# Where tiles begin in the on-chip memory, and when a small 0/1 matrix is loaded, in a one-layer hybrid decoder kernel

## The chip, the cores and the metric

The kernel runs on one core of a Trainium2 chip. A core has a matrix engine (PE, with its weight loads shown apart as PEld), three engines for elementwise work (DVE, ACT, POOL) and SP, on whose queue this kernel issues every DMA. Each engine takes its instructions in the order in which they were written into its own stream, and waits for the others by semaphores. The metric is the device time of one execution in microseconds; the kernel before took 1067.3 us (median of 3 runs, 1065.59 to 1068.7).

## The reference

The input `x` is 2048 tokens of 1024 channels. It is normalised and multiplied by one weight matrix whose 3328 columns feed four mixers of 256 channels, each with a gate:

```
h = _rms_norm(x, pre_g)
proj = jnp.einsum('bsd,de->bse', h, w_in)
aq, ak, av, ag, bu, bv, bg, cx, cg, dq, dk, dv, dg = jnp.split(proj, N_IN_SLICES, axis=-1)
ya = _dilated_mixture(heads(aq), heads(ak), heads(av))   # 4 heads, dilations 1, 4, 16
yb = _spatial_gating(bu, bv, sgu_g, sgu_w, sgu_b)
yc = _multiscale_pool(cx, pool_w, pool_scale)
yd = _retention(dq, dk, dv, ret_g)
y = jnp.concatenate([ya * jax.nn.silu(ag), yb * jax.nn.silu(bg),
                     yc * jax.nn.silu(cg), yd * jax.nn.silu(dg)], axis=-1)
y = jnp.einsum('bse,ed->bsd', y, w_out)
return x + _rms_norm(y, post_g)
```

The dilated mixture computes softmax attention three times per head (dilations 1, 4, 16) and adds the three results, each weighted per token by its share of the softmax denominators.

## The kernel before, in words

Every large product is made in three matmuls on values rounded to the matrix engine's reduced fp32 format (`F32R`): high part by high part, high by low, low by high. So an operand `x` becomes a pair: `hh` and `hl` for the normalised input (transposed, 8 blocks of 128 channels by 512 tokens), `w[:, 0]` and `w[:, 1]` for weights.

Phase 1 goes over the sequence in two halves of 1024 tokens. `prologue` normalises and transposes the half into `hh` and `hl`; then come the projections, in the order of the loop at the end of phase 1 (attention values, retention, attention queries and keys, spatial gating, pooling, attention gates). `proj_t` writes a 128-channel by 512-token block (tile `ps_t`) with `hh`/`hl` streamed through the array and weights loaded into it, 24 matmuls of 512 columns; `proj_m` writes token by channel (tile `ps_m`) with the roles swapped, matmuls of 256 columns. Results that phase 2 needs go to DRAM (`qk`, `vd`, `agd`, `yb`).

Phase 2 runs attention for two pairs of heads. `attention(p, tab)` loads queries `q2`, keys `k2a`, `k2b` and values `att_v` of a head into seven rotating buffers (tag `m8`), and `branch` works through one dilation: scores (`ps_s`), bias and row minimum on DVE (`att_p`, line 649), exponential on ACT (651), transposes into `ps_pt`, a split into `pt_hi` on ACT (658) and `pt_lo` on DVE (659), and values times probabilities (`ps_o`). `weigh` turns the three sets of row statistics into weights `wt`; it uses a small tile `eh`. `combine` spreads these weights over the 64 channels of a head by a matmul with a constant matrix of zeros and ones, `sel` (32 rows, 8 blocks of 128 columns), and sums the dilations. `out_weights` loads and splits rows of `w_out` (`wo_raw`, 128x1024). During attention of the second pair, `partial` computes the output projection of six of the eight blocks for 9 of the 16 token tiles (`ps_out`). Phase 3 finishes all 16 tiles (`final`): remaining blocks, the second normalisation, the residual, and the store.

The 0/1 matrix comes between the two pairs: two DMAs of 32x512 values into buffers of the attention probabilities (tag `pr`), each followed by a rounding copy on DVE into `sel` (lines 887 to 890).

The order on each engine isn't the order in the source: the program is recorded with a scheduler that simulates a timeline, so an instruction can be moved in its engine's stream past independent ones. Buffers are tiles of pools; a tile with a tag waits until the earlier holder of its buffer has been read for the last time. The addresses follow from the order and size of the pools: on the left side `const` (only `ident`), `big` (four buffers of 16 KB: `hh`, `hl`, later `wo` and one attention result), `small`, then the pools of a phase. So the size of `const` shifts `big` and all that follows it, and the size of `small` shifts all that follows `small`.

Of the kernel before, what the change touches and what calls it, by code (L numbers as in the profile page):

```python
# [9 lines left out]
F32 = mybir.dt.float32  # L10
F32R = mybir.dt.float32r
# [7 lines left out]
P = 128  # L19
SEQ = 2048  # L20
DM = 1024
KT = DM // P
GRP = 512
# [10 lines left out]
C_ID, C_DEC, C_ZETA, C_XI, C_CD, C_INVP, C_CNT, C_SEL, C_MIX = 0, 128, 640, 896, 1152, 1408, 1410, 1442, 2466  # L34
# [6 lines left out]
B_PR, B_PT = 6, 3  # L41
# [47 lines left out]
def hymba(ctx: ExitStack, tc: tile.TileContext, x, pre_g, w_in, sgu_g, sgu_w, sgu_b, pool_w,  # L89
          pool_scale, ret_g, w_out, post_g, cmix, catt, out, dbg=None, npart=9, spread=(0.3, 0.95)):  # L90
    nc = tc.nc
    V, A, G, T, D = nc.vector, nc.scalar, nc.gpsimd, nc.tensor, nc.sync

    def r32(ap):
        return ap.bitcast(F32)
# [7 lines left out]
    cp = ctx.enter_context(tc.tile_pool(name="const", bufs=1))  # L103
    big = ctx.enter_context(tc.tile_pool(name="big", bufs=4))
    small = ctx.enter_context(tc.tile_pool(name="small", bufs=2))
# [13 lines left out]
    ya_d = [scratch(f"ya{g}", [P, 2, GRP]) for g in range(NG)]  # L119

    ident = cp.tile([P, P], F32, name="ident")

    def rsqrt(o, v, n):

# [416 lines left out]
    p3 = ctx.enter_context(tc.tile_pool(name="p3", bufs=1, side="right", reuse_waits="tile"))  # L541
# [15 lines left out]
    def attention(p, tab):  # L557
        o01 = (big if p == 0 else po).tile([P, 2, SEQ], F32, tag="big" if p == 0 else "o01", name="att_o01")
        o2 = po.tile([P, SEQ], F32, tag="o2", name="att_o2")
        o = [o01[:, 0], o01[:, 1], o2]  # L560
        wt = pc.tile([P, 3, 2, 2, 2, 8], F32, tag="wt", bufs=1, name="wt")
        for s in range(2):
            h = 2 * p + s
            rows = slice(s * HD, (s + 1) * HD)
            other = slice((1 - s) * HD, (2 - s) * HD)
            q2 = pm.tile([P, SEQ], F32R, tag="m8", bufs=7, name="q2")
            k2a = pm.tile([P, SEQ], F32R, tag="m8", bufs=7, name="k2a")
            k2b = pm.tile([P, SEQ], F32R, tag="m8", bufs=7, name="k2b")
            D.dma_start(r32(q2[rows]), qk_d[0][p][rows, 0])
            D.dma_start(r32(q2[other]), qk_d[0][p][rows, 1])  # L570
            for z in (rows, other):
                D.dma_start(r32(k2a[z]), qk_d[1][p][rows, 0])
                D.dma_start(r32(k2b[z]), qk_d[1][p][rows, 1])
            for b, dil in enumerate(DILS):
                vt = pm.tile([P, 16, 2 * HD], F32R, tag="m8", bufs=7, name="att_v")
                dst = r32(vt)
                if dil == 1:
                    src = v_d[h].rearrange("(n t c) d -> c t n d", c=4, t=32)
                    for c in range(4):
                        D.dma_start(dst[c * 32:(c + 1) * 32], src[c])  # L580
                elif dil == 4:
                    D.dma_start(dst.rearrange("q (j c) d -> q j (c d)", j=4),
                                v_d[h].rearrange("(j q c) d -> q j (c d)", j=4, c=4))
                else:
                    D.dma_start(dst.rearrange("q r d -> q (r d)"), v_d[h].rearrange("(q r) d -> q (r d)", r=16))
                qb = q2
                if dil != 1:
                    qb = pm.tile([P, SEQ], F32R, tag="m8", bufs=7, name="q2b")
                    if dil == 4:
                        src = r32(q2).rearrange("p (j k c i) -> p c j k i", j=4, c=4, i=8)  # L590
                        dst = qb.rearrange("p (j c k i) -> p c j k i", j=4, c=4, i=8)
                        for c in range(4):
                            (V if c < 3 else G).tensor_copy(dst[:, c], src[:, c])
                    else:
                        V.tensor_copy(qb.rearrange("p (r w i) -> p r w i", r=16, i=8),
                                      r32(q2).rearrange("p (w r i) -> p r w i", r=16, i=8))
                if dil == 1:
                    sv = p2.tile([P, 3, 2, 16], F32, tag="sv", bufs=2, name="sv")
                    raw = p2.tile([64, P], F32, tag="sT", bufs=1, name="sraw")
                    D.dma_start(raw, st_d[h].rearrange("b z (n q) -> (b z n) q", q=P))  # L600
                    branch(h, dil, qb, k2a, k2b, vt, tab, o[b], sv[:, b])
                    weigh(sv, raw, wt[:, :, :, s])
                    continue
                st = p2.tile([P, 2, 16], F32, tag="stat", bufs=2, name="att_st")
                branch(h, dil, qb, k2a, k2b, vt, tab, o[b], st)
                keep_stats(h, b, dil, st)
        return o01, o2, wt
# [121 lines left out]
    def keep_stats(h, b, dil, st):  # L729

        pt = ps2.tile([P, GRP], F32, tag="t", bufs=N_T, name="ps_st")
        transpose(pt[:32, :P], st.rearrange("p z n -> p (z n)"))
        sT = p2.tile([32, P], F32, tag="sT", bufs=1, name="sT")
        V.tensor_copy(sT, pt[:32, :P])
        for z in range(2):
            dst, src = st_d[h][b, z], sT[z * 16:(z + 1) * 16]
            if dil == 4:
                for j in range(4):
                    D.dma_start(dst.rearrange("(j k c i) -> j c k i", j=4, k=16, c=4)[j],
                                src[j * 4:j * 4 + 4].rearrange("c (k i) -> c k i", i=8))  # L740
            else:
                D.dma_start(dst.rearrange("(w r i) -> r w i", r=16, i=8), src.rearrange("r (w i) -> r w i", i=8))

    def weigh(sv, raw, w):

        pt = ps2.tile([P, GRP], F32, tag="t", bufs=N_T, name="ps_sv")
        transpose(pt[:, :64], raw, 64)
        V.tensor_copy(sv[:, :2].rearrange("q b z n -> q (b z n)"), pt[:, :64])
        nm = small.tile([P, 16], F32, tag="nm", name="nm")
        V.tensor_tensor(nm, sv[:, 0, 0], sv[:, 1, 0], ALU.min)  # L750
        V.tensor_tensor(nm, nm, sv[:, 2, 0], ALU.min)
        df = small.tile([P, 3, 16], F32, tag="df", name="df")
        V.tensor_tensor(df, sv[:, :, 0], nm.unsqueeze(1).broadcast_to([P, 3, 16]), ALU.subtract)
        ew = small.tile([P, 3, 16], F32, tag="ew", name="ew")
        A.activation(ew, df, AF.Exp, scale=-1.0)
        V.tensor_tensor(df, ew, sv[:, :, 1], ALU.mult)
        V.tensor_tensor(nm, df[:, 0], df[:, 1], ALU.add)
        V.tensor_tensor(nm, nm, df[:, 2], ALU.add)
        V.reciprocal(nm, nm)
        V.tensor_tensor(ew, ew, nm.unsqueeze(1).broadcast_to([P, 3, 16]), ALU.mult)  # L760
        eh = small.tile([P, 3, 16], F32R, tag="eh", name="eh")
        V.tensor_copy(eh, ew)
        V.tensor_copy(w[:, :, :, 0], r32(eh).rearrange("q b (g n) -> q b g n", g=2))
        for b in range(3):
            V.tensor_tensor(w[:, b, :, 1], ew[:, b].rearrange("q (g n) -> q g n", g=2),
                            r32(eh[:, b]).rearrange("q (g n) -> q g n", g=2), ALU.subtract)
# [111 lines left out]
    pc = ctx.enter_context(tc.tile_pool(name="pc", bufs=1, side="right", reuse_waits="tile"))  # L878
    sel = pc.tile([32, 8, P], F32R, name="sel")
    with ExitStack() as c2:  # L880
        pm = c2.enter_context(tc.tile_pool(name="pm", bufs=1, reuse_waits="tile"))
        p2 = c2.enter_context(tc.tile_pool(name="p2", bufs=1, reuse_waits="tile"))
        ps2 = c2.enter_context(tc.tile_pool(name="ps2", bufs=2, space=PSUM, reuse_waits="tile"))
        tab = pm.tile([P, T_HEAD], F32, name="tab")
        D.dma_start(tab, catt)
        o = attention(0, tab)
        for z in range(2):
            raw = p2.tile([P, 4, P], F32, tag="pr", bufs=B_PR, name="sel_raw")[:32]
            D.dma_start(raw, cmix[:32, C_SEL + z * GRP:C_SEL + (z + 1) * GRP].rearrange("r (n m) -> r n m", m=P))
            V.tensor_copy(sel[:, z * 4:z * 4 + 4], raw)  # L890
        for i in (1, 2, 3):
            out_weights(i, V if i == 2 else G)
        combine(0, o, ps2, "t", False, range(0, SEQ, GRP), G)
        o = attention(1, tab)
        for t in range(npart):
            with tc.issue_after(marks[int(len(marks) * (t + spread[0]) / npart * spread[1])]):
                partial(t)
        out_weights(0, G)
# [13 lines left out]
    for i, t in enumerate(full):  # L912
        n = -(-len(have) // (len(full) - i))
# [30 lines left out]
```

## Time and profile before

| | |
|---|---|
| median of 3 runs | 1067.3 us (1065.59 to 1068.7) |
| the profiled execution | 1072.46 us, its span 1070.8 us |
| mean granted clock of the matrix engine | 0.977 |
| busy: PE, PEld, DVE, ACT, POOL | 95%, 81%, 49%, 35%, 21% of the span |
| HBM traffic | 127.9 MB, 119 GB/s over the span |

Phase 1 lasts to about 690 us of the span, the attention of the two head pairs to about 940, phase 3 to the end. A page lists, for each engine, busy time and groups of instructions; "idle before" is the time that the engine waited ahead of a group, with what ended the wait. The chain of waits is followed back from the last instruction: each piece ends by releasing the next. The windows view gives busy time by stretch, and the granted clock (PEclk, 1.00 is full speed). In the timeline an x behind a tile counts merged instructions, and brackets hold the idle time and its releaser. SPq rows are the issue of a DMA, not its transfer.

### The profile page before, as it was taken

Reading aid. Unit: us, or ns where it says so; the run is one execution under the profiler, and the core shown is the slowest. Engines: PE = TensorE matmul, PEld = TensorE weight load, DVE = VectorE, ACT = ScalarE, POOL = GpSimd, SP = SyncE. Lnnn points to the kernel's source line nnn. Section 1 sums busy time; section 2 is a strip of 40 time slices with the busy share of each in tenths; the row PEclk is TensorE's granted clock in tenths of the full one; section 3 lists DMA queues with packets and bytes.
Section 4 is the critical chain, followed back from the end, with each engine's and each line's share of the span. In section 5 each row is a group of like instructions: output and inputs, shape, how many; then the busy total and the mean of one; then the engine's idle time right before and its main releaser. Section 6 shows DMA issues by size and latency. Waiting matters only on the chain.

```text
span 1070.8 us, 15827 instructions
## 1 busy us (share of the span) xinstructions
PE 1013.1 (95%) x5960; PEld 862.7 (81%) x5960; DVE 521.2 (49%) x1586; ACT 377.4 (35%) x871; POOL 226.5 (21%) x216
## 2 busy tenths in 40 slices
PE   5899999999999999999999999997989989999995
PEld 5888898888777988989898777786987979866774
DVE  7511215686323331031675312177766767737766
ACT  6320213132212331132211111397763878712231
POOL 2310002121133000002120134031115521213444
PEclk9999999999999999999999999997899989999998
DMA  8530222332323232041311650286475573445566
GB/s 279 145 98 21 79 80 79 119 119 63 115 78 89 89 99 59 1 144 44 109 60 39 155 175 28 72 215 174 100 213 129 140 226 76 140 153 178 172 246 216
DMA packets 111036, 128.91 MB, mean 120 GB/s; under 512 B 9904, under 2 KB 89008, under 8 KB 108912
## 3 DMA queue, kind: packets, MB, share of 16 engines
q1 hardware_dynamic: 110960, 127.90, 40.0%
q8 instruction: 47, 0.77, 0.3%
q14 instruction: 29, 0.24, 0.1%
HBM read 91.57 MB, written 36.31 MB: 119 GB/s over the span
## 4 chain that ended last, share of the span: by engine, by line
PE 82%; DMA 9%; DVE 5%; issue 1%; POOL 1%; ACT 1%; SPq 1%; DVEq 0%; POOLq 0%; ACTq 0%
PE ps_t L98 38%; PE ps_m L98 15%; PE ps_out L98 11%; PE ps_s L98 4%; PE ps_o L98 4%; PE ps_pt L101 3%; PE ps_of L98 2%; DMA k2b<-qk 2%; DMA out_dram<-z 1%; DMA cm<-in_cmix_dram 1%; DMA z<-partd 1%; DMA sel_raw<-in_cmix_dram 1%; DMA raw<-in_w_in_dram 1%; PE ps_in L98 1%; DVE z L872 1%
## 5 line engine op out<-in xcount | busy, mean ns | idle before, releaser
L98 PE MATMUL ps_t<-hh,w 128*128 128x512 f32 x1152 | 372.8, 400 | 0.0
L98 PEld LDWEIGHTS ps_t<-hh,w 128*128 128x128 f32 x1152 | 215.9, 188 | 54.0 <-issue 3.4
L98 PE MATMUL ps_t<-hl,w 128*128 128x512 f32 x576 | 229.0, 398 | 0.0
L98 PE MATMUL ps_m<-w,hh 128*128 128x256 f32 x1024 | 187.8, 283 | 3.8 <-ACT hh L232 3.8
L98 PEld LDWEIGHTS ps_m<-w,hh 128*128 128x128 f32 x1024 | 159.1, 190 | 5.4 <-ACT hh L232 4.4
L98 PE MATMUL ps_out<-wo,yt 128*128 128x512 f32 x576 | 156.6, 411 | 0.7 <-DVE z L872 0.6
L98 PE MATMUL ps_m<-w,hl 128*128 128x256 f32 x512 | 146.4, 286 | 0.1
L98 PEld LDWEIGHTS ps_t<-hl,w 128*128 128x128 f32 x576 | 108.3, 188 | 26.1 <-issue 1.4
L98 PEld LDWEIGHTS ps_out<-wo,yt 128*128 128x128 f32 x576 | 106.6, 194 | 24.8 <-issue 2.8
L252 DVE TENSOR_TENSOR w<-raw,w 128x1024 fp32r<-128x1024 f32 x42 | 58.4, 1399 | 110.6 <-ACT w L250 110.6
L98 PEld LDWEIGHTS ps_m<-w,hl 128*128 128x128 f32 x512 | 97.3, 190 | 0.7 <-DVE hl L233 0.3
L649 DVE CUSTOM_DVE_ANT_0 att_p<-ps_s,tab 128x128 f32<-128x128 f32 (+1 forms) x192 | 60.8, 360 | 39.1 <-PE ps_s L98 32.9
L250 ACT ACTIVATE w<-raw 128x1024 fp32r<-128x1024 f32 (+1 forms) x56 | 55.0, 997 | 70.3 <-PE ps_t L98 38.2
L659 DVE TENSOR_TENSOR pt_lo<-ps_pt,pt_hi 128x512 fp32r<-128x512 f32 x80 | 51.4, 651 | 18.2 <-ACT pt_hi L658 17.6
L651 ACT ACTIVATE att_p<-att_p,att_st 128x128 f32<-128x128 f32 (+1 forms) x128 | 55.0, 432 | 10.3 <-DVE att_st L649 9.9
L98 PE MATMUL ps_o<-pt_hi,att_v 128*128 128x128 f32 (+1 forms) x204 | 52.6, 280 | 3.1 <-DVE att_o L674 3.1
L98 PE MATMUL ps_o<-pt_lo,att_v 128*128 128x128 f32 (+1 forms) x204 | 52.3, 293 | 3.3 <-DVE pt_lo L659 3.3
L101 PE MATMUL ps_pt<-ident,att_p 128*128 128x128 f32 x300 | 50.9, 286 | 1.5 <-ACT att_p L651 1.3
L446 POOL TENSOR_TENSOR d_g<-d_g,ret_b 128x512 f32<-128x512 f32 x8 | 10.4, 1294 | 185.6 <-ACT d_g L444 185.6
L658 ACT ACTIVATE pt_hi<-ps_pt 128x512 fp32r<-128x512 f32 x80 | 44.2, 565 | 12.9 <-PE ps_pt L101 7.7
L98 PEld LDWEIGHTS ps_o<-pt_hi,att_v 128*128 128x128 f32 x204 | 40.2, 197 | 5.5 <-DVE att_o L674 3.6
L98 PEld LDWEIGHTS ps_o<-pt_lo,att_v 128*128 128x128 f32 x204 | 40.2, 197 | 5.0 <-DVE pt_lo L659 3.8
(174 smaller groups left out, 1414.3 us busy)
## 6 DMA issues: line engine op xcount, KB each, us to landing
raw<-in_w_in_dram SPq DMA_DIRECT2D x52, 512.0 KB
qk<-qk_s SPq DMA_DIRECT2D x16, 512.0 KB
att_v<-vd SPq DMA_DIRECT2D x8, 1024.0 KB
xr<-in_x_dram SPq DMA_DIRECT2D x16, 512.0 KB
out_dram<-z SPq DMA_DIRECT2D x15, 512.0 KB
xt<-in_x_dram SPq DMA_DIRECT2D x7, 1024.0 KB
yraw<-yb SPq DMA_DIRECT2D x16, 384.0 KB
partd<-z SPq DMA_DIRECT2D x9, 512.0 KB
```

What stands on the lines that cost most here:

```text
L98: return T.matmul(o, lhsT, rhs, start=start, stop=stop, skip_group_check=True)
L101: T.transpose(o, i, ident[:n, :n])
L250: A.activation(hi, raw[:, :, cs], AF.Copy, scale=sc)
L252: eng.tensor_tensor(lo, raw[:, :, cs], r32(hi), ALU.subtract)
L446: G.tensor_tensor(o, o, ret_b.unsqueeze(1).broadcast_to([P, 2, 256]), ALU.mult)
L649: V.tensor_tensor_reduce(out=pr[:, u, :w], in0=ps[:, u, :w], in1=bb, scale=-SLOPES[h] * HD ** -0.5, scalar=3e38, op0=ALU.add, op1=ALU.min, ...
L651: A.activation(pr[:, u, :w], pr[:, u, :w], AF.Exp, bias=neg, scale=-1.0, accum_out=st[:, 1, n:n + 1])
L658: A.activation(hi, pt[:, :w], AF.Copy)
L659: V.tensor_tensor(lo, pt[:, :w], r32(hi), ALU.subtract)
L872: V.scalar_tensor_tensor(z[:, ns], ps, rstd, post_b[:, ns], ALU.mult, ALU.mult)
```

## The change

Three edits move tiles, one edit moves a load.

- `const` gets a tile of 384 bytes per partition that nothing uses (`align0`), `small` gets one of 32 bytes in two buffers (`align1`).
- `eh` (192 bytes, two buffers) leaves `small` for the pool `pc` on the right side, with one buffer. So `small` shrinks by 320 bytes, and what follows it is shifted by 64.
- `sel` is loaded as soon as the attention table is, by one DMA of 32x1024 values instead of two of 32x512; its buffer is one of the two `z` buffers of pool `p3`, which `wo_raw` uses too; and POOL rounds it instead of DVE.

```
     ident = cp.tile([P, P], F32, name="ident")
+    cp.tile([P, 96], F32, name="align0")
+    for _ in range(2):
+        small.tile([P, 8], F32, tag="align1", name="align1")
...
-        eh = small.tile([P, 3, 16], F32R, tag="eh", name="eh")
+        eh = pc.tile([P, 3, 16], F32R, tag="eh", bufs=1, name="eh")
...
         tab = pm.tile([P, T_HEAD], F32, name="tab")
         D.dma_start(tab, catt)
+        raw = p3.tile([P, DM], F32, tag="z", bufs=2, name="sel_raw")[:32]
+        D.dma_start(raw, cmix[:32, C_SEL:])
+        G.tensor_copy(sel, raw.rearrange("r (n m) -> r n m", m=P))
         o = attention(0, tab)
-        for z in range(2):
-            raw = p2.tile([P, 4, P], F32, tag="pr", bufs=B_PR, name="sel_raw")[:32]
-            D.dma_start(raw, cmix[:32, C_SEL + z * GRP:C_SEL + (z + 1) * GRP].rearrange("r (n m) -> r n m", m=P))
-            V.tensor_copy(sel[:, z * 4:z * 4 + 4], raw)
         for i in (1, 2, 3):
             out_weights(i, V if i == 2 else G)
```

Start addresses in a partition, as the allocator gives them, by their remainder against 512 bytes:

| tiles | before | now |
|---|---|---|
| `hh`, `hl`, `wo`, the first pair's `att_o01` | 128 | 0 |
| `xt`, `w256`, `w128`, `raw` (weights), `qk_s`, `vt`, all `p1` tiles but `c_s` | 448 | 0 |
| `q2`, `q2b`, `k2a`, `k2b`, `att_v` | 448 | 0 |
| `z4`, `xr`, `ya0`, `post_b`, final-phase `ysa` | 448 | 0 |
| `att_p`, `pt_hi`, `pt_lo` | 192 | 256 |
| `ident`; `cm`; right-side `z`, `wo_raw`, `yraw`, `yt`, `wr` | 128; 288; 480 | the same |
| `sel` | 224 | 32 |

The matrix engine's and ACT's streams are instruction for instruction what they were. On SP, where phase 1 ends and the first pair's attention has begun (`agd` stores the last gates, `wo_raw` is a block of output weights, `sga` a gate, `yraw` a block of mixer results, `att_v` values for dilation 1), before:

```order
L334 DMA agd_72<-ag_s 128x512
L550 DMA wo_raw<-in_w_out_dram 128x1024 x2
L793 DMA sga<-agd_71 128x256 x2
L813 DMA yraw<-yb_73 128x768 x2
L580 DMA att_v<-vd 32x16x128 x4
```

and now (line numbers are 3 higher, from 890 on by 2 or 3):

```order
L337 DMA agd_72<-ag_s 128x512
L890 DMA sel_raw<-in_cmix_dram 32x1024
L553 DMA wo_raw<-in_w_out_dram 128x1024
L796 DMA sga<-agd_71 128x256 x2
L816 DMA yraw<-yb_73 128x768 x2
L553 DMA wo_raw<-in_w_out_dram 128x1024
L583 DMA att_v<-vd 32x16x128 x4
```

The load of `sel` stands first, and the second `wo_raw` has moved behind `yraw`: it needs the buffer that `sel_raw` holds, so it waits until POOL has rounded `sel`. POOL's new instruction stands after the last pooling copy of phase 1 and ahead of the first rounding of `yraw`.

On DVE, where the second pair's attention begins (`q2b` reorders its queries, the first `att_st` is its first score block), before:

```order
L593 CAST q2b<-q_7287 128x4x128 x3
L659 TENSOR_TENSOR pt_lo<-ps_pt,pt_hi 128x512
L674 TENSOR_TENSOR att_o_5881<-ps_o,att_o_5881 64x512
L890 CAST sel<-sel_raw 32x512 x2
L659 TENSOR_TENSOR pt_lo<-ps_pt,pt_hi 128x512
L649 ISA att_p,att_st<-ps_s,tab 128x128
```

and now:

```order
L596 CAST q2b<-q_7287 128x4x128 x3
L662 TENSOR_TENSOR pt_lo<-ps_pt,pt_hi 128x512
L677 TENSOR_TENSOR att_o_5887<-ps_o,att_o_5887 64x512
L662 TENSOR_TENSOR pt_lo<-ps_pt,pt_hi 128x512
L652 ISA att_p,att_st<-ps_s,tab 128x128
```

The two roundings of `sel` are gone from DVE; nothing else there has moved. At the same place SP loses the two `sel_raw` loads between two loads of `att_v`, and one `yraw` now stands there instead of behind the second `att_v`.

## The prediction

> **What bounds the kernel now.** I read the chain of waits first: who ends last, by engine and by line.
>
> ```profile
> PE 82%; DMA 9%; DVE 5%; issue 1%; POOL 1%; ACT 1%; SPq 1%; DVEq 0%; POOLq 0%; ACTq 0%
> PE ps_t L98 38%; PE ps_m L98 15%; PE ps_out L98 11%; PE ps_s L98 4%; PE ps_o L98 4%; PE ps_pt L101 3%; PE ps_of L98 2%; DMA k2b<-qk 2%; DMA out_dram<-z 1%; DMA cm<-in_cmix_dram 1%; DMA z<-partd 1%; DMA sel_raw<-in_cmix_dram 1%; DMA raw<-in_w_in_dram 1%; PE ps_in L98 1%; DVE z L872 1%
> ```
>
> Four fifths of the span is the matrix engine, working. So two things can move the time: the pace of the matmuls, and the places where the chain leaves PE. One of these, `sel_raw`, belongs to this change. The chain in order of time where the second pair's attention starts (start, length, what):
>
> ```profile
> 789.41 0.23 SPq L582
> ...
> 789.70 10.04 DMA sel_raw<-in_cmix_dram
> ...
> 799.76 0.75 DVE sel L890 x2
> ...
> 800.54 0.70 DVE pt_lo L659
> ...
> 801.28 1.22 PE ps_o L98 x4
> ...
> 804.85 5.20 PE ps_out L98 x18
> 810.05 0.94 PE ps_s L98 x8
> 810.98 0.22 PE ps_w L101 x2
> ```
>
> The 0/1 matrix is loaded into a full DMA queue and takes 10.04 us. DVE meets its rounding (L890) in its own stream and waits; behind it stands the `pt_lo` for which PE waits. The timeline of DVE and of PE shows how long each stood (in brackets: idle before, releaser):
>
> ```profile
> 799.76 0.75 DVE L890 CAST sel<-sel_raw 32x512 fp32r<-32x512 f32 x2 [5.39 <-DMA sel_raw<-in_cmix_dram]
> ...
> 797.93 0.27 PE L98 MATMUL ps_o<-pt_hi,att_v 128*128 128x256 f32 x1
> 801.28 0.58 PE L98 MATMUL ps_o<-pt_lo,att_v 128*128 128x256 f32 x1 [3.08 <-DVE pt_lo L659]
> ```
>
> PE had other matmuls to run until 798.2 and then lost 3.08 us. It lost more after that. The windows view (stretch, length, busy time of PE, PEld, DVE, ACT, POOL, granted clock, DMA share, GB/s):
>
> ```profile
> 57.80:97.00 39.20, 39.20 (x171) 31.58 (x170) 6.18 (x9) 6.54 (x10) 3.42 (x3) 1.00 0.23 67
> 97.00:119.60 22.60, 22.60 (x194) 22.60 (x193) 0.69 (x1) 1.79 (x3) 0.00 (x0) 1.00 0.01 1
> 694.90:697.60 2.70, 2.70 (x14) 2.70 (x14) 1.31 (x7) 2.70 (x12) 0.00 (x0) 0.50 1.01 309
> 702.70:703.60 0.90, 0.90 (x10) 0.90 (x9) 0.90 (x7) 0.90 (x2) 0.90 (x1) 1.00 1.13 279
> 801.30:806.90 5.60, 5.60 (x21) 5.12 (x22) 5.47 (x24) 4.78 (x18) 0.00 (x0) 0.50 0.16 64
> 806.90:812.00 5.10, 5.10 (x29) 4.28 (x28) 4.33 (x19) 2.25 (x9) 3.04 (x4) 1.00 0.10 39
> ```
>
> After the gap PE worked for 5.60 us without a pause, but at a granted clock of 0.50; from 806.9 it was back at 1.00. Half of that stretch, 2.8 us, is a second price of the same stall.
>
> **The later load of the matrix: what its removal is worth.** On PE's side, 3.08 us of gap and 2.8 us of half clock: 5.9 us. On DVE's side, the next `pt_lo` started at 800.54. Without the wait it needs only its `pt_hi`, from ACT:
>
> ```profile
> 794.80 0.98 ACT L658 ACTIVATE pt_hi<-ps_pt 128x512 fp32r<-128x512 f32 x2 [1.15 <-PE ps_pt L101]
> ```
>
> Two in 0.98 us, so the first is there at about 795.4 and DVE runs 5.1 us earlier. DVE was busy 5.47 of the 5.60 us behind the stall, and 4.33 of the 5.10 after it: with PE at full clock the two run about even, and DVE's 5.1 may be the shift that counts, since `ps_w` at 810.98 needs DVE's weights. I take the middle of 5.1 and 5.9, 5.5. The ends: nothing, if something else is late at once, and 8.9 us, if all of DVE's wait and casts (5.39 + 0.75) and the 2.8 of half clock come back.
>
> What is late next? The values of the new head, issued just ahead of `sel_raw`:
>
> ```profile
> 789.26 0.39 SPq L582 DMA_DIRECT2D att_v<-vd  x1
> 789.70 1.87 SPq L889 DMA_DIRECT2D sel_raw<-in_cmix_dram  x2
> ```
>
> Their first `ps_o` comes on PE after the 18 `ps_out` that ended at 810.05. Moved up by 5.9 us, that is 804.1, still later than 799.7, when the small load issued behind these values had landed. So they stop nobody. Further on the chain stays on PE until PE releases a key buffer and waits for its refill:
>
> ```profile
> 863.40 0.49 PE ps_o L98 x4
> ...
> 864.03 7.03 DMA k2b<-qk
> ```
>
> That load starts when PE is done with the buffer, so it moves up with PE. I pass the 5.5 us on to the end whole.
>
> **The early load: what it costs.** In its new place the load is first on SP, where `wo_raw` was (SP's issues, then two windows):
>
> ```profile
> 692.30 0.89 SPq L550 DMA_DIRECT2D wo_raw<-in_w_out_dram  x2
> 700.92 1.92 SPq L580 DMA_DIRECT2D att_v<-vd  x4
> ...
> 688.00:692.00 4.00, 3.25 (x17) 2.53 (x15) 0.64 (x4) 1.24 (x2) 0.00 (x0) 1.00 0.02 4
> 692.00:696.00 4.00, 3.23 (x18) 2.83 (x19) 1.54 (x9) 3.99 (x13) 0.00 (x0) 0.78 0.73 215
> ```
>
> The DMA engines were idle before it (share 0.02), and the next 4 us moved 215 GB/s, 0.86 MB; so its 128 KB, first in the queue, should land by 696, an estimate from these two rows. POOL then rounds 1024 columns. No row has that size; POOL's casts do 384 and 512 columns (the groups), and POOL and ACT do this around then (the timeline):
>
> ```profile
> L825 POOL CAST yt<-yraw 128x384 fp32r<-128x384 f32 x18 | 9.0, 505 | 127.8 <-PE ps_out L98 84.6 <-DMA yraw<-yb 32.8 <-issue 9.9
> L593 POOL CAST q2b<-q 128x512 fp32r<-128x512 f32 x4 | 2.6, 645 | 25.9 <-DMA q<-qk 13.4 <-PE ps_s L98 12.4
> ...
> 700.76 0.95 POOL L825 CAST yt<-yraw 128x384 fp32r<-128x384 f32 x2 [32.75 <-DMA yraw<-yb]
> 703.08 1.99 ACT L551 ACTIVATE wo<-wo_raw 128x1024 fp32r<-128x1024 f32 x2
> ```
>
> 140 ns more for 128 columns, so 645 + 4 x 140 = 1.2 us, between 0.65 and, at twice that, 1.3. POOL had been idle for 32.75 us before 700.76, so this lies in free time. The second `wo_raw` is then issued at about 697.2, 3.7 us ahead of the `att_v` loads that stand behind it, and its 512 KB, at the 215 GB/s above, should be there by 700 to 702: ACT takes it second, at about 704.1. I count nothing. If the cover is gone, each us by which POOL's rounding ends after 700.9 holds SP, and with it `att_v` and later the keys of the next head, for which the chain already waits:
>
> ```profile
> 722.00 9.33 DMA k2b<-qk
> ```
>
> The ends are 0 and 3 us.
>
> `eh` with one buffer: its writer and its readers are DVE instructions in order, so no wait comes of it. The fillers issue nothing.
>
> **The addresses: does the pace of a matmul depend on them?** Before, not one of the large operands begins on a multiple of 256 or 512, so the trace has no aligned case. It has several unaligned ones, and I ask whether they differ, and whether the lost time looks like a matter of place. Pieces of the chain, and how many such matmuls there are:
>
> ```profile
> 57.81 39.20 PE ps_t L98 x168
> 97.01 22.61 PE ps_m L98 x192
> 694.90 0.85 PE ps_s L98 x4
> 702.71 0.94 PE ps_s L98 x8
> ...
> L98 PE MATMUL ps_t<-hh,w 128*128 128x512 f32 x1152 | 372.8, 400 | 0.0
> L98 PE MATMUL ps_m<-w,hh 128*128 128x256 f32 x1024 | 187.8, 283 | 3.8 <-ACT hh L232 3.8
> L98 PE MATMUL ps_out<-wo,yt 128*128 128x512 f32 x576 | 156.6, 411 | 0.7 <-DVE z L872 0.6
> ```
>
> At clock 1.00 a 512-column matmul takes 39.20/168 = 233 ns (it streams `hh`, start 128), a 256-column one 22.61/192 = 118 ns (it streams `w256`, start 448). The `ps_s` of 694.90, of 256 columns (start 448), ran at clock 0.50: 0.85/4 = 213 ns. Twice the clock should make it 106; `ps_m` gives 118. So a tenth of the pace is missing at full clock; the loss is in proportion to the columns and the same for both starts; and at half clock, with tiles as unaligned, it isn't seen. The `ps_s` of 702.71 stream 128 columns at a step of four values, so over as many bytes as a 512-column matmul, 2048: 118 ns. If each crossing of a 512-byte boundary cost time, these would lose as much as that one does, 233 less 2 x 106, some 20 ns; they lose 11 over 106. So the loss goes with streaming time, not with bytes crossed: a limit of the reading rate, which a new start leaves alone. I take 0. The ends: all of it back, with 1728 `ps_t` (the low half adds 576), 1536 `ps_m` (adds 512) and 768 `ps_out` (`ya` and `ysa` add 192): 1728 x 20 + 1536 x 11 + 768 x 20 ns = 67 us; and as a loss, a quarter more of the same shortfall, 17 us.
>
> [...]
>
> DMAs: 9% of the span, 96 us, is DMA on the chain; about half of it (`k2b`, `out_dram`, `z`, `raw`) moves tiles that are now aligned. A 4096-byte row from 448 touches nine blocks of 512 bytes, an aligned one eight. If time went by blocks, 48/9 = 5 us would be saved. I count 0, with 5 us as either end.
>
> **Sum.** -5.5 + 0 + 0 on a span of 1070.8 in an execution of 1072.46, which was 0.5% above the median shown, 1067.3. From the median that leaves 1061.8; I say 1062.
>
> **Rivals.**
>
> *The gain is swallowed.* The wait of 5.39 us is of one execution with a crowded queue; or `ps_w` and the following key loads wait in its place. For it: DVE is as full as PE there. Against: the chain runs on PE from 801 to 863. Time: 1064 to 1068.5, the median less 0 to 3.
>
> *Alignment pays on the matmuls.* For it: a tenth of the pace is missing and every operand is unaligned. Against: the three paces above. Half of the 67 us with the stall's 5.5 gives about 1028, a tenth of it 1055.
>
> *Alignment pays on the DMAs*, by the blocks above: 5 us and the stall's 5.5, about 1057. Against: DMA on the chain is mostly waiting in a shared queue. [...]
>
> *Slower.* Streamed and loaded operands now begin in the same phase of 512 bytes, where before they were 320 apart (128 and 448); if the two reads of the array collide more often so, every product pays. Place: `ps_t`, `ps_m`, `ps_out`, in columns as much as 3264 matmuls of 512. It cancels the gain at 5.5 us / 3264 = 1.7 ns a matmul and shows as slower from 2.7 ns; at a quarter more of the shortfall, 5 ns, the 16 us give 1078. Against: `ps_t` and `ps_m` swap the roles of 128 and 448 and run at one pace.
>
> **Chances.** The forecast (1059 to 1064) 0.52; swallowed 0.20; matmuls 0.10; DMAs 0.06; slower 0.12. With the slower case and most of the matmul case left out, the range is 1048 to 1069. A measurement of this kernel can't tell 0.3% (3.2 us) from no change: faster than that has 0.68, within it 0.20, slower 0.12.
>
> **What would show it.** Right: no wait of DVE on `sel_raw`, and no gap on PE with a half clock behind it where the second pair begins; POOL's rounding of `sel` ending before 700; `att_v` for dilation 1 issued at about 701; pieces of `ps_t` still at 233 ns and of `ps_m` at 118. Wrong: `ps_t` near 216 or above 236; an SP that stands on the second `wo_raw`; a new wait of PE near 800 as long as the old one.

## The result and the profile after

The changed kernel takes 1059.26 us (median of 8 runs, 1055.14 to 1063.4) where the kernel before takes 1067.48 (8 runs, 1064.02 to 1069.69). The ratio is 0.9924, 95% interval [0.9903, 0.9945]: 8.1 us faster. The number lies inside the predicted range, 3 us under the predicted 1062. The reasons behind it were largely wrong, so the number came out by luck: the addresses, which I counted at nothing, account for the gain, and the load of the 0/1 matrix, which I counted at 5.5 us, adds nothing beside them that the times can show.

The profiled execution of the changed kernel is the fastest of its eight (1055.14), that of the kernel before 5 us over its median. So these two executions differ by 17.3 us, twice what the medians do, and I compare directly only what should not depend on the execution: the pace of a kind of matmul at full clock.

The two pieces of the chain of waits from which the prediction read the paces (start, length, what), and the groups that they belong to, in the changed kernel:

```profile
55.91 38.13 PE ps_t L98 x168
94.03 23.03 PE ps_m L98 x192
...
L98 PE MATMUL ps_t<-hh,w 128*128 128x512 f32 x1152 | 366.9, 395 | 0.0
L98 PE MATMUL ps_m<-w,hh 128*128 128x256 f32 x1024 | 190.1, 286 | 1.6 <-ACT hh L235 1.6
```

`ps_t` went from 39.20 to 38.13 us for the same 168 matmuls, from 233.3 to 227.0 ns each; its group fell by 5.9 us. `ps_m` went the other way, from 22.61 to 23.03 us for 192, from 117.8 to 119.9 ns, and its group grew by 2.3. Both were at clock 1.00, as the windows of the changed kernel show:

```profile
55.90:94.00 38.10, 38.10 (x171) 31.52 (x170) 6.18 (x9) 6.52 (x10) 3.42 (x3) 1.00 0.24 69
94.00:117.00 23.00, 23.00 (x194) 23.00 (x193) 0.69 (x1) 1.79 (x3) 0.00 (x0) 1.00 0.01 1
```

The load of the matrix does what the prediction said of it. SP's issues and POOL's timeline in the changed kernel:

```profile
683.40 0.38 SPq L890 DMA_DIRECT2D sel_raw<-in_cmix_dram  x1
683.84 0.41 SPq L553 DMA_DIRECT2D wo_raw<-in_w_out_dram  x1
...
688.25 0.33 SPq L553 DMA_DIRECT2D wo_raw<-in_w_out_dram  x1
690.54 2.24 SPq L583 DMA_DIRECT2D att_v<-vd  x4
...
687.19 1.03 POOL L891 CAST sel<-sel_raw 32x1024 fp32r<-32x1024 f32 x1 [27.38 <-ACT att_p L654]
```

POOL rounds it in 1.03 us of free time, done at 688.2; the second `wo_raw`, for which SP stands 0.3 us until POOL is done, is issued right behind, 2.3 us ahead of `att_v`; DVE no longer waits for `sel`.

### The profile page after: what moved, and what is told of

Same layout as the page of the kernel before. It is cut to its first block, busy times and chain, and to the rows that moved or that the text cites. A ratio compares the mean times of both kernels' runs of the same rounds, so it can differ in the third digit from the quotient of the medians.

```text
span 1053.4 us, 15825 instructions
## 1 busy us (share of the span) xinstructions
PE 1000.1 (95%) x5960; PEld 861.6 (82%) x5960; DVE 519.1 (49%) x1584; ACT 376.4 (36%) x871; POOL 228.0 (22%) x217
## 4 chain that ended last, share of the span: by engine, by line
PE 82%; DMA 7%; DVE 6%; ACT 2%; issue 2%; POOL 1%; SPq 1%; DVEq 0%; POOLq 0%; ACTq 0%
PE ps_t L98 38%; PE ps_m L98 16%; PE ps_out L98 10%; PE ps_s L98 4%; PE ps_o L98 4%; PE ps_pt L101 3%; PE ps_of L98 2%; DMA out_dram<-z 2%; DMA k2b<-qk 2%; DMA cm<-in_cmix_dram 1%; PE ps_in L98 1%; POOL z L877 1%; PE ps_mix L98 1%; DMA raw<-in_w_in_dram 1%; PE ps_x L101 1%
## 5 line engine op out<-in xcount | busy, mean ns | idle before, releaser
L98 PE MATMUL ps_t<-hh,w 128*128 128x512 f32 x1152 | 366.9, 395 | 0.0
L98 PE MATMUL ps_t<-hl,w 128*128 128x512 f32 x576 | 226.1, 393 | 0.0
L98 PE MATMUL ps_m<-w,hh 128*128 128x256 f32 x1024 | 190.1, 286 | 1.6 <-ACT hh L235 1.6
L98 PEld LDWEIGHTS ps_m<-w,hh 128*128 128x128 f32 x1024 | 161.3, 193 | 3.3 <-ACT hh L235 2.2
L98 PE MATMUL ps_out<-wo,yt 128*128 128x512 f32 x576 | 153.9, 406 | 0.6 <-DVE z L875 0.6
L877 POOL TENSOR_TENSOR z<-z,xr 128x1024 f32<-128x1024 f32 x15 | 35.8, 2390 | 32.4 <-DVE z L875 27.7
```

Of the source, the lines that this page charges most:

```text
L98: return T.matmul(o, lhsT, rhs, start=start, stop=stop, skip_group_check=True)
L877: (V if last else G).tensor_tensor(z[:, ns], z[:, ns], xr[:, ns], ALU.add)
```

## The experiments

A start below is the remainder against 512 bytes; the distance is the start of the tile that is loaded as weights less the start of the tile that is streamed. Pace is the mean time between the starts of successive matmuls of a kind, without the pairs that are more than 6% off.

**The matrix alone, the addresses alone.** The first kernel takes the new load and leaves all starts as they were, the second the reverse.

```
e1_sel_only
+        raw = p3.tile([P, DM], F32, tag="z", bufs=2, name="sel_raw")[:32]
+        D.dma_start(raw, cmix[:32, C_SEL:])
+        G.tensor_copy(sel, raw.rearrange("r (n m) -> r n m", m=P))
...
-        for z in range(2):
...
e2_align_only
+    cp.tile([P, 96], F32, name="align0")
+    for _ in range(2):
+        small.tile([P, 8], F32, tag="align1", name="align1")
...
+        eh = pc.tile([P, 3, 16], F32R, tag="eh", bufs=1, name="eh")
```

> Only the load of the 0/1 matrix is moved (early, one DMA, rounded by POOL); no fillers, eh stays in its pool, so every address is as before. The theory that the stall near 800 us is worth what the trace of before shows: PE keeps 233 ns for a 512-column ps_t and 118 ns for a 256-column ps_m, DVE no longer waits for sel_raw, and the time is 5 to 6 us under the kernel before (ratio about 0.995). The rival that this stall was larger in the profiled execution than it usually is: same paces, no wait in the trace, but the time is within 2 us of the kernel before.

> Only the addresses are changed (both fillers, eh moved); the 0/1 matrix is loaded late and rounded by DVE as before. The theory that the paces seen in the changed kernel come from the addresses: ps_t 227 ns, ps_m 120 ns, ps_out 227 to 228 ns in the last phase; 1728 x 6.3 ns less 1536 x 2.1 ns plus some 490 x 5.6 ns make 10.4 us at most, so a ratio of 0.990 to 0.993; DVE waits for sel_raw as before. The rival that the paces come from the order of the instructions or from the chip: 233 and 118 ns, ratio 1.00.

Both against the same 23 runs of the kernel before (median 1067.57): the matrix alone 1066.92, ratio 0.9976 [0.9959, 0.9994]; the addresses alone 1059.28, ratio 0.9902 [0.9873, 0.9931]. So the first is worth 0.7 us by the medians and 2.6 by the ratio, less than the 5 to 6 expected, and the second 8.3 and 10.5. The paces follow the addresses: 233.4 and 117.8 ns with the matrix alone, 227.8 and 119.8 with the addresses alone. With the late load kept, DVE still waits for the matrix, but for 3.0 us instead of 5.39 (the tile `sel_raw` in the kernel with the addresses alone, then the window that holds PE's gap):

```profile
L893 DVE CAST sel<-sel_raw x2: 408/412/415, 784.2 to 784.6; 32x512 fp32r<-32x512 f32 x2
...
  DVE sel L893: 3.0, 1
...
784.90:787.00 2.10, 1.39 (x11) 1.22 (x10) 2.07 (x9) 1.04 (x5) 0.00 (x0) 1.00 0.93 372
```

PE loses 0.7 us there (2.10 less 1.39) instead of 3.08, and the clock is 1.00, as it is in the 10 us that follow. The half clock that I priced at 2.8 us does not belong to this stall in every execution.

**Is it the multiple of 512, or the distance of two starts?** Three kernels with the early load and other fillers. The first (e3 from here on) has `hh`, `hl` and `wo` at 0 and leaves the rest at 448; the second (e4) leaves those at 128 and puts the rest at 0; the third (e5) puts all of them at 448.

```
e3_streams0
+    cp.tile([P, 96], F32, name="align0")
...
+        eh = pc.tile([P, 3, 16], F32R, tag="eh", bufs=1, name="eh")
...
e4_rest0
+    for _ in range(2):
+        small.tile([P, 8], F32, tag="align1", name="align1")
...
e5_both448
+    cp.tile([P, 80], F32, name="align0")
+    for _ in range(2):
+        small.tile([P, 8], F32, tag="align1", name="align1")
...
+        eh = pc.tile([P, 3, 16], F32R, tag="eh", bufs=1, name="eh")
```

> The early load of the 0/1 matrix, and hh, hl, wo at 0 against 512 bytes, all that follows at 448 as before. So ps_t streams from 0 and loads weights from 448; ps_m streams from 448 and loads from 0; ps_out of the last phase streams from 0 and loads from 448 (yt, ysa, ya). If the start of the streamed operand alone sets the pace: ps_t 227. If the start of the loaded operand alone sets it: ps_t 233, ps_out 233, ps_m 120. If the distance of the two sets it (ps_t 192 before, 0 now, here 64): ps_t and ps_m need not equal either value, and ps_m (distance 448, before 320) may go another way than ps_t.

> The early load of the 0/1 matrix, hh, hl, wo at 128 as before, and all that follows at 0. So ps_t streams from 128 and loads from 0; ps_m streams from 0 and loads from 128; ps_out of the last phase streams from 128 and loads from 0. If the start of the loaded operand alone sets the pace: ps_t 227, ps_out 227, ps_m 118. If the start of the streamed one alone does: ps_t 233, ps_m 120. If the distance does (ps_t 128, ps_m 384): values of their own.

> The early load of the 0/1 matrix, and all of hh, hl, wo, w256, w128 at 448: streamed and loaded operand share a phase, but not 0. If only the distance of the two counts, as at (0,0): ps_t 227, ps_m 120. If the start of hh, hl, wo at 0 is what helps: ps_t and ps_out back at 233 or another value of their own.

The chains of the three, in this order:

```profile
57.52 38.47 PE ps_t L98 x168
95.99 21.78 PE ps_m L98 x192
```

```profile
57.37 39.19 PE ps_t L98 x168
96.56 23.04 PE ps_m L98 x192
```

```profile
55.80 38.11 PE ps_t L98 x168
93.91 23.03 PE ps_m L98 x192
```

With none of these operands on a multiple of 512 or 256, the third has the paces of the changed kernel: 38.11 and 23.03 against 38.13 and 23.03. So the multiple is not what counts. And the second, whose weights lie at 0, gains next to nothing. What orders them is the distance, taken modulo 256 (where a cell has two paces, each stretch of `ps_m` ran at one or the other):

| kernel | `ps_t`: distance, pace | `ps_m`: distance, pace | median us, ratio to before |
|---|---|---|---|
| before | 64, 233.4 | 192, 117.8 | |
| changed | 0, 227.8 | 0, 119.8 | 1059.26, 0.9924 [0.9903, 0.9945] |
| e3 | 192, 229.3 | 64, 113.3 or 117.8 | 1056.04, 0.9868 [0.9836, 0.9901] |
| e4 | 128, 232.7 | 128, 118.6 or 120.0 | 1066.42, 0.9974 [0.9953, 0.9994] |
| e5 | 0, 227.7 | 0, 119.7 | 1050.39 (one run; before 1066.44) |

**A map of the distance.** This kernel computes nothing of the reference and returns rows of `x`. After loading, it runs groups of 24 matmuls in the pattern of `ps_t`, and of 48 in that of `ps_m`, with the streamed tile shifted by a to h (0 to 448 bytes in steps of 64) and the loaded one by A to H.

```
for s in range(8):
    for l in range(8):
        wide(s * 16, l * 16, ...)     # 512 columns streamed from S, weights from W
...
        narrow(s * 16, l * 16, ...)   # 256 columns streamed from W2, weights from S
```

> Measures the disputed cost by itself. It computes nothing of the reference (it copies a part of x to the output) and times groups of 24 matmuls, 48 for the narrow form, in the order of proj_t (512 columns, weights of 128 columns) and of proj_m (256 columns, loaded operand in steps of 512 columns), for each start of the streamed operand and each start of the loaded one, in steps of 64 bytes against 512, and some in odd steps of 32. If the start of the streamed operand alone sets the pace, rows of this map are constant; if that of the loaded one alone, columns; if only the distance counts, diagonals. From the kernels run so far (streamed, loaded): 512 columns (128,448) 233, (0,0) 227.6, (0,448) 229, (128,0) 232.5; 256 columns (448,128) 118, (0,0) 119.8, (448,0) 114.6, (0,128) 119 to 120. The rival, that it is something else of these kernels (other engines, DMAs, where the tiles lie beyond 512 bytes), expects other paces at these eight points.

Pieces of its chain (first letter the streamed start, second the loaded one), distances 0, 64, 128, 192, 0, then two of another streamed start, then the narrow ones:

```profile
35.18 5.21 PE wide_aA L42 x23
40.40 5.60 PE wide_aB L42 x24
45.99 5.58 PE wide_aC L42 x24
51.57 5.51 PE wide_aD L42 x24
57.08 5.45 PE wide_aE L42 x24
...
167.75 5.59 PE wide_dA L42 x24
...
184.43 5.45 PE wide_dD L42 x24
...
389.11 5.75 PE narrow_aA L42 x48
394.86 5.66 PE narrow_aB L42 x48
400.51 5.70 PE narrow_aC L42 x48
406.21 5.66 PE narrow_aD L42 x48
```

`wide_dD` has the 5.45 us of `wide_aE`, and `wide_dA`, with the loaded start 192 below the streamed one (so 64 above it modulo 256), 5.59, within 0.01 the 5.60 of `wide_aB`. All 64 pairs follow the distance modulo 256: 227.2 ns at 0, 233.4 at 64, 232.3 at 128, 229.3 at 192 for 512 columns; 119.9, 117.8, 118.6 and 117.8 for 256. With one of the two starts shifted by another 32 bytes, 512 columns take 233 to 234 at any distance. These are the paces of the kernels in the table but for one: 256 columns at distance 64, where e3 shows 113.3 as well.

**How much of the lost time is the load of the weights?** Again nothing of the reference: the same groups with weights of 128, 64 or 32 columns (`all`, `two`, `one`), the distances A to D.

```
for m, mn in ((128, "all"), (64, "two"), (32, "one")):
    w0 = W[:, lo + k * P:lo + k * P + m]
```

> Leaves the reference out, as m1_map did, and times groups of 24 matmuls with 512 or 256 streamed columns, 128, 64 or 32 loaded columns, and the loaded operand 0, 64, 128 or 192 bytes behind the streamed one, each group twice. If the shortfall against 213 ns (106 ns) is the stream waiting while a weight load reads, it falls with the loaded columns: with 128 columns 227, 233, 232, 229 ns as before, with 64 some 8 to 12 ns over 213, with 32 some 4 to 8. If it is a limit of the reading rate of the stream, as the prediction had it, to which the distance only adds: 227 or more for 128, 64 and 32 columns alike.

Its chain, with all and with a quarter of the weights, for 512 columns at distance 0 and at 64 and for 256 at 64:

```profile
36.44 5.21 PE wide_all_Ax L42 x23
...
47.09 5.60 PE wide_all_Bx L42 x24
...
124.71 5.56 PE wide_one_Ax L42 x24
...
135.82 5.56 PE wide_one_Bx L42 x24
...
174.88 2.83 PE half_all_Bx L42 x24
...
219.25 2.72 PE half_one_Bx L42 x24
```

With a quarter of the weights the distance hardly matters any more: 230.0 to 231.7 ns over the four distances for 512 columns (226.7 to 233.4 with all of them), 113.3 at each for 256. So the part that depends on place hangs on the load as well as on the stream: its spread for 512 columns fell from 6.7 to 1.7 ns. A smaller load does not always help, though. For 256 columns it is faster at every distance (24 matmuls in 2.72 to 2.80 us, with all the weights in 2.83 to 2.88); for 512 columns it is faster at distance 64 (5.56 to 5.59 us against 5.60) and slower at distance 0, where a quarter of the weights takes 231.7 ns and all of them 226.7. A smaller load also writes fewer rows of the result (64 or 32 instead of 128), which this kernel does not separate. And both expectations missed: the pace did not fall towards 213, and it was not the same for all loads. No group went below 226.7 and 113.3 ns. In the kernel before, at a granted clock of 0.50, 512 columns took 427.2 ns (`ps_out`) and 256 columns 213.4 (`ps_m`), from which I estimate 213.6 and 106.7 at twice that clock: the other 6%, some 13 of the 20 ns that `ps_t` lacked, came back at no distance and with no load.

**A version with the two distances chosen apart.** The changed kernel with two more fillers, ahead of `w256` and behind it, so that `w256` begins at 448 and `w128` stays at 0: `ps_t` keeps distance 0, `ps_m` gets 64.

```
+                if not shifted:
+                    pa.tile([P, 112], F32, name="align2")
...
+                if not shifted:
+                    pa.tile([P, 16], F32, name="align3")
+                    shifted.append(1)
```

> The changed kernel with two more fillers around w256, so that it begins at 448: ps_t, ps_out of the last phase as in the changed kernel (both operands at 0, distance 0, best of the 512-column map), ps_m as in e3 (w256 at 448, hh at 0, distance 64). By the map: ps_t 227, ps_m 118, which is 1536 x 2.1 = 3.2 us less than the changed kernel, a ratio of 0.987 to 0.990. If ps_m runs at 113 in most groups, as in e3, 8 to 10 us less: 0.982 to 0.985. The rival, that PE's pace in ps_m is covered by something else, expects 0.992 as for the changed kernel.

1052.85 us against 1066.45, ratio 0.9863 [0.9837, 0.9888], 13.6 to 14.6 us under the kernel before; its interval lies wholly below that of the changed kernel. Its chain shows `ps_t` at the pace of the changed kernel and `ps_m` in two paces:

```profile
57.01 38.11 PE ps_t L98 x168
95.12 22.61 PE ps_m L98 x192
...
141.19 21.97 PE ps_m L98 x192
```

22.61 us for 192 is 117.8 ns. The 21.97 hold a first group that is slower in each kernel (118.2 ns here, 124.2 in the changed one) and seven at 113.3; the changed kernel took 23.23 for this piece. Over all of `ps_m` the mean pace fell from 119.8 to 115.6 ns, 1536 x 4.2 = 6.5 us, close to the difference of the two medians (1059.26 less 1052.85 = 6.4), which were not taken side by side.

**Two paces at one distance.** In e3 and the version above, stretches of `ps_m` with equal addresses ran at either pace. This kernel computes nothing of the reference; it enters groups of 256 columns behind two matmuls (`lead`) of other widths, or behind such a pair after PE has stood idle. Beside it e3 was profiled a second time, unchanged.

```
for n in (0, 32, 64, 96, 160, 192, 224, 512):
    if n: lead(n, "lead")
    group(d * 16, P, 256, ...)        # distance 0, 64, 128, 192
```

> Computes nothing of the reference; its output is a copy of rows of x. Groups of 24 matmuls of 256 columns with weights of 128 columns, at the four distances 0, 64, 128, 192 bytes (A to D), each entered in other ways: directly behind another group, behind two matmuls of 32, 64, 96, 160, 192, 224 or 512 columns, or after the matrix engine has stood idle. It asks why products at distance 64 ran at 117.8 ns in some projections and at 113.3 in others, with the same addresses. Theory: two steady paces exist at this distance, and the way a stretch is entered picks one; then the B groups show both values here, each group holding its own for its whole length. Rival: the values or something else of the kernel decide; then all B groups stay at 117.8 as in the first map, A at 119.9, C at 118.6, D at 117.8.

> The kernel with hh, hl and wo at 0 and all else at 448, profiled a second time. If the program alone picks the pace of a projection, the same three of the twelve stretches of 256 columns (the one at about 222 and the one at 424 us) run at 117.8 and the others at 113.3, as in the first profile; if the moment at which a stretch begins picks it, others do. ps_t again 229 ns. Time 1050 to 1058.

Its chain at distance 64, behind leads of 224 and of 512 columns; and a stretch of `ps_m` in the first and in the second profile of e3:

```profile
77.30 0.22 PE lead L42 x2
77.52 2.83 PE half_B_after L42 x24
80.35 0.47 PE lead L42 x2
80.82 2.73 PE half_B_after L42 x24
```

```profile
221.94 9.74 PE ps_m L98 x81
```

```profile
221.86 9.41 PE ps_m L98 x81
```

At distance 64 a group ran at 117.7 to 117.8 directly behind another group and behind leads of 160 and 224 columns, and at 113.2 to 113.4 in its second half behind all others and after idling. Each keeps its pace once it has settled. At 192 one group of eleven did the same; at 0 none, and at 128 the pace moves between 118 and 120. In e3 the stretch at 222 us ran at 117.8 in one execution and 113.3 in the other, the one at 550 the other way round, with the same program and addresses. Here the first gap of the stretch differed by 3 ns between the two executions (226 and 223, 203 and 200), and each had settled within six matmuls. So how a stretch is entered picks the pace in the kernel that tests it; that this is also what differs between the executions of e3 fits these gaps, but is not shown. What decides which entry leads to which pace stays open.

**Does the early load add to the addresses?** The changed kernel and the one with the addresses alone once more, side by side.

> The changed kernel itself, timed beside the one with the addresses alone, on one chip. The two parts measured singly were -2.6 us (the early load) and -10.5 us (the addresses), together -13.1, and the whole was measured at -8.1. Theory: the parts add, and the whole was measured on the slow side of its spread; then this is 2 to 3 us below the addresses alone, some -11 to -13 against the kernel before. Rival: once the addresses have moved everything earlier, the late load no longer stands in the way (its wait of DVE was 3.0 us there, with 0.7 us of gap on the matrix engine); then the two are within 1.5 us of each other. A third: the early load costs something next to the aligned tiles; then this is slower than the addresses alone by 1.5 us or more.

> The addresses alone, the 0/1 matrix loaded late as before: the other half of the pair. -8 to -11 us against the kernel before by every theory; what counts is its difference to the changed kernel: 2 to 3 us above it if the parts add, within 1.5 us if the late load stands in nobody's way any more, 1.5 us or more below it if the early load costs.

The changed kernel took 1058.96 us, 0.9923 [0.9896, 0.9949], the addresses alone 1057.70, 0.9919 [0.9896, 0.9941]. The two lie 1.3 us apart, with the early load the slower, and the intervals leave room for 3 to 4 us either way; the 5.5 us of the prediction lie outside. The traces show where the gain of a stall that is really gone can be lost. First the late load in the chain of the kernel with the addresses alone (rows between left out):

```profile
777.88 7.99 DMA sel_raw<-in_cmix_dram
785.89 0.75 DVE sel L893 x2
...
794.86 1.03 DVE eh L765
...
796.32 0.38 PE ps_w L101 x2
```

From the stall to `ps_w` the chain runs over DVE, which was busy for 10.69 of the 11.1 us between the end of its wait, at 785.89, and 797. From 773 to 793 us, instruction against instruction, the changed kernel gained 1.9 us on this one, and 1.5 to 1.9 in each of the four pairings of their two executions. Behind the place most of that went again. The load of the next keys in the chain of the kernel with the addresses alone, and then in the changed one:

```profile
848.77 6.76 DMA k2b<-qk
```

```profile
847.73 6.90 DMA k2b<-qk
```

In this pair (the changed kernel in its first execution) PE was 2.1 us ahead at 830 us, but the load started only 1.0 us earlier. SP issues it directly behind `sraw`, which reads the row statistics back from DRAM: in the four executions SP stands 3.1 to 4.4 us there until `std` has stored them, and at most 0.3 us more for PE. PE then waits 3.6 to 4.1 us for the keys. In each of the four pairings 1.0 to 1.9 us went between 830 and 860 us, so that of the gain from 0.5 us to nothing was left.

Ahead of the place the changed kernel had lost as well (here in its second execution). The load of the keys, and PE behind it, in the kernel with the addresses alone and then in the changed one:

```profile
713.02 9.30 DMA k2b<-qk
722.46 1.62 PE ps_s L98 x6
```

```profile
713.99 9.12 DMA k2b<-qk
723.24 1.62 PE ps_s L98 x6
```

At 672 us the changed kernel had been 0.5 us ahead; here it is 0.8 behind, and at 755, 4.0 behind. The windows (clock in the third column from the end) tell where the rest went, the addresses alone first:

```profile
685.00:725.00 40.00, 31.74 (x217) 28.87 (x217) 25.99 (x115) 37.21 (x125) 8.24 (x7) 0.85 0.86 221
725.00:770.00 45.00, 43.18 (x306) 39.15 (x305) 38.79 (x132) 38.16 (x116) 7.84 (x6) 0.98 0.49 133
```

```profile
685.00:725.00 40.00, 31.33 (x212) 28.62 (x213) 24.82 (x111) 35.97 (x120) 9.28 (x8) 0.82 0.90 222
725.00:770.00 45.00, 42.79 (x281) 38.94 (x281) 37.54 (x122) 35.34 (x110) 7.81 (x6) 0.90 0.43 113
```

The clock withheld 40 x 0.15 + 45 x 0.02 = 6.9 us in the one and 40 x 0.18 + 45 x 0.10 = 11.7 in the other, counted as if PE had always had work. In the other two executions it was 5.0 (addresses alone) and 8.7 (changed). Both executions with the early load lost more than both without. But the load alone does not do it: by the same sum e5 and the version with two distances, which load early too, lost 6.9 and 5.2. What does stays open.

## Why the prediction was right in its number and wrong in its reasons

- **The late load, 5.5 us.** Mis-sized. Alone it is worth 0.7 us by the medians, 2.6 [0.6, 4.4] by the ratio; beside the new addresses nothing. In the traces the part was there: the kernel with the matrix alone is 1.2 us ahead of the kernel before at 776 us and 5.65 at 816, so 4.5 came from this place, and in that pair it was still there at 900 (SP stood 2.2 us on `std` there, 3.5 in the kernel before). What failed is the step "it moves up with PE. I pass the 5.5 us on to the end whole". Three things were wrong with it. The 5.39 us and the 2.8 us of half clock were those of one execution, 5 us above the median; with the addresses alone the wait was 3.0 and 3.4 us and the clock did not fall. The next key load hangs on `std` and `sraw` as well as on PE, and in four pairings it took back 1.0 to 1.9 of 1.5 to 1.9 us. And the key loads and the clock of the first pair, ahead of the place, vary by more than the gain. "The gain is swallowed" (0.20), which named the following key loads, is what became of this term.
- **The early load, 0.** Right at its place: 1.03 us on POOL (1.2 estimated), 0.3 us for which SP stands, the issues in the order said. What it costs between 672 and 755 us is not settled: the four pairings of executions above give 0.1 to 6.3 us, the clock included.
- **The matmuls, 0.** This is the larger step that failed: "a limit of the reading rate, which a new start leaves alone". I compared starts, 128 against 448, where the difference of two starts counts; and I compared 512 columns at distance 64 with 256 columns at distance 192, which by the map lie at 233.4 and 2 x 117.8 = 235.6 for reasons of their own. The same 512 columns at the other distance, 229.3, would have shown it, and the trace had no such case. The third reading carries nothing either: it holds 128 columns of `ps_s` against 106 ns, which is worked out from 256 columns; by columns it would be 53. In the same trace the 128 columns of `ps_pt` take 0.33 us for three, 110 ns each, so at this width neither goes by its columns, and 118 cannot be read as a loss of 11. What the runs show in place of the step, for the changed kernel: 1728 `ps_t` x 5.6 ns = 9.7 us gained, 1536 `ps_m` x 2.0 = 3.1 lost, 408 `ps_out` of the last phase x 5.7 = 2.3 gained, and 360 whose `yt` still begins at 480 (an odd multiple of 32 from `wo`), x 0.9 = 0.3. Together 9.2 us, against 8.3 to 10.5 measured for the addresses alone. Two thirds of the step stand: 13 of the 20 ns came back at no start that was tried. So "alignment pays on the matmuls" (0.10) came nearest, at a seventh of its 67 us, though not by alignment: e5 has the same paces with none of these operands aligned.
- **"Slower", by streams and loads in one phase.** The rival asked about the right quantity, the two starts against each other, but the sign depends on the columns: distance 0 costs 256 columns 2.0 ns and spares 512 columns 5.6.
- **The DMAs, 0.** The DMA queues' share of the engines times the span is 418 to 423 us in the six executions whose tiles behind `small` begin at 0 (the changed kernel, the addresses alone, e4, the version with two distances but for its `w256`) and 425 to 433 in the five where they begin at 448 (before, the matrix alone, e3, e5). So the DMA engines seem to be busy some 2% less, a clean but narrow split: the two of e3 alone are 432 and 425. No piece of the chain shows a gain from it: at 40 us the changed kernel is 1.9 us ahead of the one before, but so, by 1.7, is the one with the matrix alone, whose tiles have not moved.
- **What would show it.** Of the signs named, the pieces of `ps_t` and `ps_m` answered: 227, neither 233 nor "near 216", a pace that no run shows: the fastest group of 512 columns took 226.7 ns a matmul. The time alone, 3 us beside the forecast, would have hidden that: 5.5 us that did not come and some 9 that were not forecast nearly cancel. That is luck.

## What to carry to other kernels

Where a kernel is bound by its matmuls at full clock, the distance between the start of the streamed and of the loaded operand is a setting to try, for each shape by itself: a few unused bytes between tiles moved these matmuls by 1 to 4%, and the best distance of one shape was the worst of the other (in the map, at distance 0, 227.2 ns for 512 columns and 119.9 for 256). A price read off one stall in one execution is an upper end, above all where it includes a half clock, until the stall is taken away alone and timed; and what waits next has to be followed back to all that it waits for, not to the engine that ends last in one trace. And when equal paces are offered as evidence that a place doesn't matter, the cases have to differ in what may matter and in nothing else.

## What the runs showed of the hardware

- In the map, the pace of fp32r matmuls with 128 by 128 weights at clock 1.00 depends on (loaded start less streamed start) modulo 256 bytes: 227.2, 233.4, 232.3, 229.3 ns for 512 columns at 0, 64, 128, 192, and 233 to 234 where the two differ by an odd multiple of 32; 119.9, 117.8, 118.6, 117.8 for 256. What PE streams and what it loads bear on each other: with a quarter of the weights 256 columns ran at 113.3 ns at every distance (in the map, with all of them, 117.8 to 119.9), and for 512 columns the spread over the distances fell from 6.7 to 1.7 ns, around 231. By what mechanism stays open.
- At distance 64, 256 columns ran at one of two paces with equal addresses, 113.3 or 117.8 ns, and in the kernel that tests it the way a stretch is entered picked one.
- The best pace seen of these matmuls, 226.7 ns for 512 columns and 113.3 for 256, is 6% above half of what they took at a granted clock of 0.50 in the kernel before (427.2 / 2 = 213.6 and 213.4 / 2 = 106.7), in proportion to the columns; no distance and no size of the load went below it. What it is stays open.
